# A hybrid decoder block on one core: Silu as one instruction, eight row buffers, and a rewritten passage between the projections and the up projections

## The chip, the core and the metric

The kernel runs on one core of a Trainium2 chip. A core has a matrix engine (PE, with PEld for its weight loads), a vector engine (DVE), a scalar engine that evaluates functions (ACT), GpSimd (POOL), and a sync engine (SP) that here only issues transfers. ACT issues transfers too: a transfer that stands in ACT's instruction list takes its turn there, and what stands behind it waits. Each engine works through its own list in order; semaphores join the lists. The metric is the device time of one execution in microseconds (us), as the median of several runs.

## What is computed

One layer over 16 meta tokens and 1024 real ones, D_MODEL 1024, everything float32:

```python
h = rmsnorm(concat([meta, x]), norm_g)
u_pool, z_pool, q, k, v, z_attn, f_logit, g_pool, g_attn = split(h @ w_in)
y_pool = causal_multiscale_pool(u_pool, pool_w, pool_scale) * silu(z_pool)
y_attn = forgetting_attention(q, k, v, log_sigmoid(f_logit + b)) * silu(z_attn)
merged = sigmoid(g_pool) * (y_pool @ w_up_pool) + sigmoid(g_attn) * (y_attn @ w_up_attn)
out = rmsnorm(x + merged @ w_out, final_norm_g)[meta rows dropped]
```

The pooling mixer takes, for each of four groups of 128 channels, a trailing mean over 2, 4, 8 or 16 positions minus the token itself, and then a 128x128 map. The attention has 8 heads of 64 channels; its softmax is divided by its row sums at the end.

## The kernel before

Matrix work is done on float32 split into a high and a low part, so each product takes three matmuls (`g_mm3`): high by high, high by low, low by high. A "raw" column block (`f_raw`, L281) is one of 24 blocks of 128 projected channels (four for each of `za` and `zp`, eight for each of `gp` and `ga`): 48 matmuls in two halves of 24, and each half is evicted from PSUM by an ACT copy into a staging tile `st` (L288) and stored to DRAM by SP (L289). Their PSUM tiles come from a pool of three, `pj`, so a half can begin only when the half three before it has been evicted. `f_u` stores the pooling input in the same way.

Attention fills the first two thirds of the time, with projections woven in as filler. Twenty raw blocks fit in there. The last four (`ga4` to `ga7`, the list `left`) run behind it and are PE's only work while the other engines prepare what the up projections need. This passage, L686 to L805, is where the change lies. In it:

- `reload` (L695) brings a stored row of z back from DRAM on ACT's queue, into a buffer of the tag "b", of which there are five.
- `silu_of` (L700) is a reload, a Sigmoid on ACT (L703) and a product on POOL (L704).
- `pool_pre` (L743) loads `u` on SP (L745), forms the window sums on DVE (L753, one to four adds) and the difference (L759), and splits it into `plh` (ACT, L762) and `pll` (DVE, L763). `pool_mm` (L715) runs 6 matmuls, then a DVE product with the gated z (L721), an ACT copy `yh` (L722) and a POOL difference `yl` (L723).
- The row sums are loaded, inverted (L728) and stored to DRAM as `recs`. `attn_out` (L731) loads the attention output `y` and two broadcast rows of reciprocals `rc` (L733, L737, both on ACT's queue), multiplies on DVE (L738), and gates on POOL (L740). L803 (ACT) and L804 (DVE) split the gated rows into `yah` and `yal`.
- `up(j, a)` (L820) loads and splits a weight block into `whu` (ACT, L826) and `wlu` (DVE, L827), reloads and squashes the gate, and runs 24 matmuls; `a` is 0 for the pooling branch, 1 for attention. The order is up(0,0), then up(j+1,0) and up(j,1) in turn.

PE's order is the order of the code. On the other engines a scheduler places the instructions by what they depend on; `after(ins, prev)` (L103) adds a dependence that only orders two instructions. In the kernel before, every Sigmoid is held behind the last Exp, so that ACT changes its function table once.

Of the kernel before, what the change touches and what calls it, by code (L numbers as in the profile page):

```python
# [8 lines left out]
F32 = mybir.dt.float32  # L9
# [5 lines left out]
D = 1024  # L15
# [39 lines left out]
def tile_hybrid_block(ctx, tc, x, meta, norm_g, w_in, b_forget, pool_w, pool_scale,  # L55
# [223 lines left out]
    spill = {}  # L279

    def f_raw(key, col):  # L281
        w = w_chunk(col)
        dt = dr.tile([128, SEQ], F32, name=f"sp_{key[0]}{key[1]}")
        spill[key] = dt
        for c0, c1 in HALVES:
            ps = yield from g_proj(w, NM + c0, NM + c1)
            st = stg.tile([128, 512], F32, name="st")
            nc.scalar.activation(st, ps, AF.Copy)  # L288
            nc.sync.dma_start(dt[:, c0:c1], st)  # L289
# [194 lines left out]
    pw = sm.tile([128, 4, 128], F32, name="pw", bufs=1)  # L484
# [197 lines left out]
    last_exp, last_dve = exps[-1], dves[-1]  # L682
# [6 lines left out]
    def after_exp(ins):  # L689
        after(ins, last_exp)  # L690

    def btile(name, dt=F32, tag="b"):
        return bp.tile([128, SEQ], dt, name=name, tag=tag, bufs=8 if tag == "y" else 5)
# [6 lines left out]
    def silu_of(key):  # L700
        z = reload(key)
        sg_ = btile("sg")
        after_exp(nc.scalar.activation(sg_, z, AF.Sigmoid))  # L703
        nc.gpsimd.tensor_tensor(z, z, sg_, op=ALU.mult)  # L704
        return z
# [9 lines left out]
    def pool_mm(zp, g, plh, pll):  # L715
        yh = btile("yh", F32R, "y")
        yl = btile("yl", F32R, "y")
        for c0, c1 in HALVES:
            ps = bank()
            run(g_mm3(ps, [(pwh[:, g], pwl[:, g], plh[:, c0:c1], pll[:, c0:c1])]))  # L720
            nc.vector.scalar_tensor_tensor(zp[:, c0:c1], ps, psc[:, g:g + 1], zp[:, c0:c1], op0=ALU.mult, op1=ALU.mult)  # L721
            nc.scalar.activation(yh[:, c0:c1], zp[:, c0:c1], AF.Copy)  # L722
            nc.gpsimd.tensor_tensor(yl[:, c0:c1], zp[:, c0:c1], r32(yh[:, c0:c1]), op=ALU.subtract)  # L723
        ypl[g] = (yh, yl)

    lall = sm.tile([128, 64], F32, name="lall", bufs=1)
    nc.sync.dma_start(lall, sums.rearrange("h (a b) -> (h a) b", b=64))
    nc.vector.reciprocal(lall, lall)  # L728
    nc.sync.dma_start(recs.rearrange("h (a b) -> (h a) b", b=64), lall)

    def attn_out(p):  # L731
        y = gp.tile([128, SEQ], F32, name="y", tag="g")
        nc.scalar.dma_start(y, spill["y", p])  # L733
        rc = btile("rc")
        for e in range(2):
            h = 2 * p + e
            nc.scalar.dma_start(rc[rows(e)[0]], recs[h:h + 1, :].to_broadcast([64, SEQ]))  # L737
        nc.vector.tensor_tensor(y, y, rc, op=ALU.mult)  # L738
        zs = silu_of(("za", p))
        nc.gpsimd.tensor_tensor(y, y, zs, op=ALU.mult)  # L740
        Y[p] = y

    def pool_pre(g):  # L743
# [16 lines left out]
        plh = gp.tile([128, SEQ], F32R, name="plh", tag="g")  # L760
        pll = gp.tile([128, SEQ], F32R, name="pll", tag="g")
        nc.scalar.activation(plh, u[:, NM:], AF.Copy)  # L762
        nc.vector.tensor_tensor(pll, u[:, NM:], r32(plh), op=ALU.subtract)  # L763
        return g, plh, pll

    made = [pool_pre(3), pool_pre(2)]
# [6 lines left out]
    def pooled():  # L773
        g, plh, pll = made.pop(0)
        pool_mm(zps.pop(0), g, plh, pll)

    zps = [silu_of(("zp", 3))]
    run(left[0])
    made.append(pool_pre(1))
    zps.append(silu_of(("zp", 2)))  # L780
    run(left[1])
    pooled()
    attn_out(0)
    made.append(pool_pre(0))
    zps.append(silu_of(("zp", 1)))
    run(left[2])
    pooled()
    attn_out(1)
    zps.append(silu_of(("zp", 0)))
    half_raw(left[3])  # L790
    pooled()
    pooled()
    run(left[3])
    attn_out(2)
    attn_out(3)
    HX.close()
    hq = ctx.enter_context(tc.tile_pool(name="hq", bufs=16, side="right", reuse_waits="tile"))

    ya = []
    for k in range(4):  # L800
        yh = hq.tile([128, SEQ], F32R, name="yah", tag="h")
        yl = hq.tile([128, SEQ], F32R, name="yal", tag="h")
        nc.scalar.activation(yh, Y[k], AF.Copy)  # L803
        nc.vector.tensor_tensor(yl, Y[k], r32(yh), op=ALU.subtract)  # L804
        ya.append((yh, yl))  # L805

    wo = {}

    def wo_chunk(k):
        raw = wp.tile([128, D], F32, name="rawo", tag="raw")  # L810
        nc.sync.dma_start(raw, wout[:, k, :])
        hi = hq.tile([128, D], F32R, name="woh", tag="h")
        lo = hq.tile([128, D], F32R, name="wol", tag="h")
        nc.scalar.activation(hi, raw, AF.Copy)
        nc.vector.tensor_tensor(lo, raw, r32(hi), op=ALU.subtract)
        wo[k] = (hi, lo)

    mg, gt = [], {}

    def up(j, a):  # L820
        y = (ypl, ya)[a]
# [7 lines left out]
        after_exp(nc.scalar.activation(sg_, sg_, AF.Sigmoid))  # L829
# [16 lines left out]
    up(0, 0)  # L846
    for j in range(8):
        if j < 7:
            up(j + 1, 0)
        up(j, 1)  # L850
# [77 lines left out]
```

## Time and profile before

| | |
|---|---|
| median of 3 runs | 799.39 us (798.90 to 800.28) |
| the profiled execution | 798.15 us, its span 796.40 us |
| PE busy | 765.2 us, 96% |
| DVE, ACT, POOL busy | 477.1, 394.7, 303.4 us |
| mean granted PE clock | 0.984 |

By stage (busy us in each stretch of the span):

| us from the start | PE | DVE | ACT | POOL | PE clock |
|---|---|---|---|---|---|
| 0 to 25, norm and first projections | 17.80 | 14.51 | 14.53 | 14.91 | 0.86 |
| 25 to 530, attention with filler | 502.60 | 329.43 | 286.01 | 194.23 | 1.00 |
| 530 to 571, first half of the passage | 41.00 | 27.68 | 13.95 | 16.71 | 1.00 |
| 571 to 612, second half of the passage | 25.64 | 23.65 | 18.06 | 37.70 | 0.87 |
| 612 to 701, up projections | 89.00 | 48.64 | 39.94 | 20.99 | 0.98 |
| 701 to 797, output projection | 89.13 | 33.21 | 22.21 | 18.82 | 0.97 |

How to read such rows: a timeline row gives the start, the duration, the engine, the line, the operation, output and input by the program's names, how many instructions the row joins, and in square brackets how long the engine had been idle before it and what ended that. A group row gives the least, the median and the greatest duration in nanoseconds. A PE row's end is modelled and laps over the next row's start, so distances are best taken from start to start. Rows with ACTq or SPq are the issuing of transfers, not their moving. The profiled execution is 1.75 us longer than its span, and 1.24 us shorter than the median.

### The profile page before, as it was taken

What the parts mean: (1) busy time and instruction counts of PE and PEld (TensorE: products, weight loads), DVE (VectorE), ACT (ScalarE), POOL (GpSimd) and SP (SyncE); (2) the same over time, 40 slices, a digit from 0 to 9 for tenths busy, and PEclk for the clock granted to TensorE, in tenths of its full rate; (3) what the DMA queues carried; (4) which work ended last, traced back from release to release, by engine and by line L of the source; (5) the groups of instructions that cost most, each with busy time, mean ns of one, the idle gap of its engine ahead of it and who ended that gap; (6) DMA issues with size and microseconds to landing.
All of it is one profiled execution on the core that took longest, in us unless ns stands there. A gap on an engine that the chain in (4) does not pass through costs nothing.

```text
span 796.4 us, 10658 instructions
## 1 busy us (share of the span) xinstructions
PE 765.2 (96%) x3893; PEld 653.1 (82%) x3893; DVE 477.1 (60%) x759; ACT 394.7 (50%) x755; POOL 303.4 (38%) x244
## 2 busy tenths in 40 slices
PE   6999999999999999999999999999695999999996
PEld 5897999988889888898888888888573888888885
DVE  4843566558568676586586675687637555434232
ACT  6652456457557564584475455643345445232121
POOL 5511225326316334253163172445588122222111
PEclk9999999999999999999999999999998999999998
DMA  9301122311321312313213223235474654533331
GB/s 298 90 5 51 28 90 71 94 53 47 92 68 27 86 47 68 86 34 85 86 43 99 74 67 87 73 113 188 165 257 135 198 181 162 185 106 106 106 107 53
DMA packets 74068, 79.86 MB, mean 100 GB/s; under 512 B 5504, under 2 KB 56704, under 8 KB 74016
## 3 DMA queue, kind: packets, MB, share of 16 engines
q1 hardware_dynamic: 68048, 59.79, 24.6%
q10 hardware_dynamic: 5968, 19.40, 7.7%
q8 instruction: 30, 0.49, 0.3%
q14 instruction: 22, 0.18, 0.1%
HBM read 58.10 MB, written 21.07 MB: 99 GB/s over the span
## 4 chain that ended last, share of the span: by engine, by line
PE 86%; DMA 5%; DVE 3%; issue 2%; POOL 2%; ACT 1%; SPq 0%; ACTq 0%; POOLq 0%; DVEq 0%
PE pj L140 61%; PE pj L862 11%; PE po L596 5%; PE ps L531 2%; PE ps L530 2%; DMA rl<-sp_za 2%; DVE s L753 1%; PE pj L446 1%; DMA u<-sp_u 1%; PE pt L551 1%; PE pt L559 1%; DMA gb<-in_norm_g_dram 1%; DMA y<-sp_y 1%; POOL rl L704 1%; POOL yl L723 1%
## 5 line engine op out<-in xcount | busy, mean ns | idle before, releaser
L140 PE MATMUL pj<-hh,whi 128*128 128x512 f32 (+4 forms) x768 | 183.0, 365 | 8.5 <-ACT st L288 6.0
L140 PE MATMUL pj<-hh,wlo 128*128 128x512 f32 (+4 forms) x768 | 180.1, 361 | 0.0
L140 PE MATMUL pj<-hl,whi 128*128 128x512 f32 (+4 forms) x768 | 179.7, 361 | 0.0
L129 POOL TENSOR_TENSOR wlo<-raw,whi 128x1024 fp32r<-128x1024 f32 x37 | 91.2, 2465 | 231.5 <-ACT whi L128 92.3
L140 PEld LDWEIGHTS pj<-hh,whi 128*128 128x128 f32 x768 | 132.3, 191 | 26.8 <-ACT st L288 6.5
L140 PEld LDWEIGHTS pj<-hl,whi 128*128 128x128 f32 x768 | 132.6, 190 | 17.9
L140 PEld LDWEIGHTS pj<-hh,wlo 128*128 128x128 f32 x768 | 131.9, 189 | 16.8
L580 DVE TENSOR_TENSOR pl<-S,ph 128x512 fp32r<-128x512 f32 (+4 forms) x112 | 93.8, 850 | 16.2 <-ACT ph L579 15.2
L588 POOL TENSOR_TENSOR acc<-acc,S 128x272 f32<-128x272 f32 (+4 forms) x80 | 77.1, 964 | 13.7 <-ACT S L576 8.3
L539 ACT ACTIVATE S<-ps,negc 128x400 f32<-128x400 f32 (+2 forms) x96 | 49.4, 515 | 55.3 <-DVE S L537 48.3
L575 DVE TENSOR_TENSOR S<-S,pt 128x512 f32<-128x512 f32 (+4 forms) x112 | 49.9, 498 | 21.4 <-PE pt L559 21.3
L576 ACT ACTIVATE S<-S 128x512 f32<-128x512 f32 (+4 forms) x112 | 48.5, 476 | 25.8 <-DVE S L575 25.7
L579 ACT ACTIVATE ph<-S 128x512 fp32r<-128x512 f32 (+4 forms) x112 | 52.8, 479 | 13.8 <-PE po L596 13.1
L546 DVE TENSOR_TENSOR m<-m,S 128x272 f32<-128x272 f32 (+4 forms) x80 | 40.6, 508 | 19.9 <-ACT S L539 18.2
L862 PE MATMUL pj<-wol,gh 128*128 128x512 f32 (+1 forms) x136 | 51.8, 381 | 0.0
L862 PE MATMUL pj<-woh,gh 128*128 128x512 f32 (+1 forms) x136 | 51.8, 381 | 0.0
L862 PE MATMUL pj<-woh,gl 128*128 128x512 f32 (+1 forms) x136 | 51.7, 380 | 0.0
L842 POOL TENSOR_TENSOR gl<-rl,gh 128x512 fp32r<-128x512 f32 x16 | 22.6, 1413 | 72.7 <-ACT gh L841 72.6
L128 ACT ACTIVATE whi<-raw 128x1024 fp32r<-128x1024 f32 x37 | 39.0, 1055 | 17.4 <-PE pj L140 16.1
L838 DVE TENSOR_TENSOR rl<-pj,rl 128x512 f32<-128x512 f32 x32 | 21.9, 688 | 35.1 <-PE pj L140 31.6
L288 ACT ACTIVATE st<-pj 128x512 f32<-128x512 f32 x48 | 28.4, 591 | 24.3 <-PE pj L140 23.8
L596 PE MATMUL po<-pl,V 128*128 128x512 f32 (+4 forms) x112 | 37.5, 335 | 0.0
(166 smaller groups left out, 1174.1 us busy)
## 6 DMA issues: line engine op xcount, KB each, us to landing
raw<-in_w_in_dram SPq DMA_DIRECT2D x40, 512.0 KB, 4.1
sp_gp<-st SPq DMA_DIRECT2D x16, 256.0 KB, 2.1
sp_ga<-st SPq DMA_DIRECT2D x16, 256.0 KB, 2.0
rl<-sp_gp ACTq DMA_DIRECT2D x8, 512.0 KB, 3.5
rl<-sp_ga ACTq DMA_DIRECT2D x8, 512.0 KB, 4.9
rawo<-in_w_out_dram SPq DMA_DIRECT2D x8, 512.0 KB, 4.8
xr<-in_x_dram SPq DMA_DIRECT2D x8, 512.0 KB, 4.3
xt<-in_x_dram SPq DMA_DIRECT2D x7, 512.0 KB
```

The lines of the kernel that those rows point to most:

```text
L128: nc.scalar.activation(hi, raw, AF.Copy)
L129: (eng or nc.gpsimd).tensor_tensor(lo, raw, r32(hi), op=ALU.subtract)
L140: nc.tensor.matmul(ps, a, b, start=(i == 0), stop=(i == len(seq) - 1))
L539: nc.scalar.activation(s[:kb, f0:], ps[:kb, f0:], AF.Identity, bias=nb_)
L546: nc.vector.tensor_tensor(m[:kb, c0:], m[:kb, c0:], s[:kb, c0:], op=ALU.max)
L575: nc.vector.tensor_tensor(s[:kb, c0:], s[:kb, c0:], self.pm[:kb, c0:], op=ALU.subtract)
L576: exps.append(nc.scalar.activation(s[:kb, c0:], s[:kb, c0:], AF.Exp))
L579: nc.scalar.activation(ph[:kb, c0:], s[:kb, c0:], AF.Copy)
L580: dves.append(nc.vector.tensor_tensor(pl[:kb, c0:], s[:kb, c0:], r32(ph[:kb, c0:]), op=ALU.subtract))
L588: nc.gpsimd.tensor_tensor(acc[:kb, c0:], acc[:kb, c0:], s[:kb, c0:], op=ALU.add)
L596: nc.tensor.matmul(self.po[:, c0:], v, r[:kb, c0:], start=(b == 0 and i == 0), stop=(b == self.nb - 1 and i == 1))
L862: nc.tensor.matmul(ps[:, :c1 - c0], mg[k][a][:, r], wo[k][b][:, c0:c1], start=(k == 0 and n == 0), stop=(k == KO - 1 and n == 2))
```

## The change

- **Silu.** `silu` is one ACT instruction in place. The Sigmoid on ACT with a POOL product, and the tile between them, are gone: eight products fewer on POOL. Silu and Sigmoid are not in one function table, so the built program has one more table load on ACT.
- **Buffers.** The tag "b" has eight buffers. All eight z rows (`zp`, `za`) are loaded ahead of the raw blocks, on ACT's queue. `pw`, a staging tile of the pooling map, now shares the attention tile `t`'s buffer.
- **Order of evictions.** Every Silu, gate Sigmoid and `plh` copy is held behind the latest eviction that was emitted before it (`evacs[-1]`) instead of behind the last Exp. `pool_pre` is cut into `pool_chain` and `pool_split`, placed between halves of raw blocks.
- **Attention rows.** `y` is loaded on SP early (`attn_in`) and gated on POOL first (`attn_gate`). The products with the reciprocals and the splits (`attn_out`) come behind up(0,0), and the eight `rc` loads go to SP, held behind the last store of the raw blocks.
- **Up projections.** Weights are loaded in a call of their own (`up_weights`), for the first two ahead of time, and the order is up(0,0), up(1,0), then up(j+2,0) and up(j,1) in turn: one more pooling block ahead of the first attention block.

```diff
 def f_raw(key, col):
-            nc.scalar.activation(st, ps, AF.Copy)
-            nc.sync.dma_start(dt[:, c0:c1], st)
+            evacs.append(nc.scalar.activation(st, ps, AF.Copy))
+            stores.append(nc.sync.dma_start(dt[:, c0:c1], st))
...
-    pw = sm.tile([128, 4, 128], F32, name="pw", bufs=1)
+    pw = ap_.tile([128, 4, 128], F32, name="pw", tag="t")
...
-        return bp.tile([128, SEQ], dt, name=name, tag=tag, bufs=8 if tag == "y" else 5)
+        return bp.tile([128, SEQ], dt, name=name, tag=tag, bufs=8)
...
-    def silu_of(key):
-        z = reload(key)
-        sg_ = btile("sg")
-        after_exp(nc.scalar.activation(sg_, z, AF.Sigmoid))
-        nc.gpsimd.tensor_tensor(z, z, sg_, op=ALU.mult)
-        return z
+    def silu(z):
+        after(nc.scalar.activation(z, z, AF.Silu), evacs[-1])
...
+    def attn_in(p):
+        y = gp.tile([128, SEQ], F32, name="y", tag="g")
+        nc.sync.dma_start(y, spill["y", p])
+        Y[p] = y
+
+    def attn_gate(p, zs):
+        ins = nc.gpsimd.tensor_tensor(Y[p], Y[p], zs, op=ALU.mult)
+        if p > 1:
+            after(ins, yls[-1])
+
     def attn_out(p):
-        y = gp.tile([128, SEQ], F32, name="y", tag="g")
-        nc.scalar.dma_start(y, spill["y", p])
         rc = btile("rc")
         for e in range(2):
             h = 2 * p + e
-            nc.scalar.dma_start(rc[rows(e)[0]], recs[h:h + 1, :].to_broadcast([64, SEQ]))
-        nc.vector.tensor_tensor(y, y, rc, op=ALU.mult)
-        zs = silu_of(("za", p))
-        nc.gpsimd.tensor_tensor(y, y, zs, op=ALU.mult)
-        Y[p] = y
+            after(nc.sync.dma_start(rc[rows(e)[0]], recs[h:h + 1, :].to_broadcast([64, SEQ])), stores[-1])
+        nc.vector.tensor_tensor(Y[p], Y[p], rc, op=ALU.mult)
+        yh = hq.tile([128, SEQ], F32R, name="yah", tag="h")
+        yl = hq.tile([128, SEQ], F32R, name="yal", tag="h")
+        nc.scalar.activation(yh, Y[p], AF.Copy)
+        nc.vector.tensor_tensor(yl, Y[p], r32(yh), op=ALU.subtract)
+        ya.append((yh, yl))
...
+    def pool_split(g):
+        u, plh, pll = chains[g]
+        after(nc.scalar.activation(plh, u[:, NM:], AF.Copy), evacs[-1])
+        return nc.vector.tensor_tensor(pll, u[:, NM:], r32(plh), op=ALU.subtract)
...
+    for p in range(3):
+        attn_in(p)
+    half_raw(left[0])
+    pool_split(3)
+    run(left[0])
+    split2 = pool_split(2)
+    silu(zp[3])
+    silu(zp[2])
+    lall = sm.tile([128, 64], F32, name="lall", bufs=1)
...
+    pool_chain(1)
+    half_raw(left[1])
+    silu(zp[1])
+    silu(zp[0])
+    run(left[1])
+    pooled(3)
+    silu(za[0])
+    silu(za[1])
+    attn_gate(0, za[0])
+    pool_split(1)
+    pool_chain(0)
+    attn_in(3)
+    half_raw(left[2])
+    silu(za[2])
+    silu(za[3])
+    attn_gate(1, za[1])
+    run(left[2])
+    pooled(2)
+    pool_split(0)
+    half_raw(left[3])
+    first_up = up_weights(0, 0)
+    pooled(1)
+    pooled(0)
+    run(left[3])
+    attn_gate(2, za[2])
...
+    attn_gate(3, za[3])
+    second_up = up_weights(1, 0)
...
-    up(0, 0)
+    up(0, 0, first_up)
+    for p in range(4):
+        attn_out(p)
+    up(1, 0, second_up)
     for j in range(8):
-        if j < 7:
-            up(j + 1, 0)
-        up(j, 1)
+        if j < 6:
+            up(j + 2, 0, up_weights(j + 2, 0))
+        up(j, 1, up_weights(j, 1))
```

The scheduler decides what this makes of the lists. Two places show it.

ACT's list in the last raw blocks, before. The three `st` rows are the evictions of `ga4`'s second half and of `ga5`'s two halves:

```order
L288 ACTIVATE st<-pj 128x512
L762 ACTIVATE plh<-u 128x1024
L697 DMA rl<-sp_zp_3066 128x1024
L733 DMA y<-sp_y_755 128x1024
L288 ACTIVATE st<-pj 128x512
L703 ACTIVATE sg<-rl 128x1024
L737 DMA rc<-recs 64x1024
L762 ACTIVATE plh<-u 128x1024
L288 ACTIVATE st<-pj 128x512
```

Between the last two of them stand a Sigmoid, a transfer of reciprocals and the split of a window sum.

The same place of ACT's list in the change; the three `st` are the two halves of `ga5` and the first of `ga6`:

```order
L288 ACTIVATE st<-pj 128x512
L698 ACTIVATE rl<-rl 128x1024 x2
L128 ACTIVATE whi<-raw 128x1024
L288 ACTIVATE st<-pj 128x512
L698 ACTIVATE rl<-rl 128x1024 x2
L715 ACTIVATE yh<-rl 128x512 x2
L762 ACTIVATE plh<-u 128x1024
L694 DMA rl<-sp_gp_3785 128x1024
L694 DMA rl<-sp_gp_3914 128x1024
L288 ACTIVATE st<-pj 128x512
```

`ga5`'s second eviction now has two Silu and a weight split ahead of it; the `plh` split and the wait that it brings stand behind it, ahead of `ga6`'s first eviction.

DVE's list around the first up projection, before: the products with the reciprocals (`y<-y,rc`) and a split of the attention rows stand ahead of up(0,0)'s `wlu`:

```order
L738 TENSOR_TENSOR y<-y,rc 128x1024
L721 SCALAR_TENSOR_TENSOR rl<-pj,psc,rl 128x512 x6
L738 TENSOR_TENSOR y<-y,rc 128x1024 x2
L804 TENSOR_TENSOR yal<-y,yah 128x1024
L827 TENSOR_TENSOR wlu<-rawu,whu 128x512
L804 TENSOR_TENSOR yal<-y,yah 128x1024 x3
L827 TENSOR_TENSOR wlu<-rawu,whu 128x512
```

And in the change, from the first product with a reciprocal on; the `wlu` of up(0,0), up(1,0) and up(2,0) all stand ahead of it, and one `rl<-pj,rl` and then the `wlu` of up(0,1) follow the last row:

```order
L734 TENSOR_TENSOR y<-y,rc 128x1024
L806 TENSOR_TENSOR rl<-pj,rl 128x512
L738 TENSOR_TENSOR yal<-y,yah 128x1024
L734 TENSOR_TENSOR y<-y,rc 128x1024
L806 TENSOR_TENSOR rl<-pj,rl 128x512
L734 TENSOR_TENSOR y<-y,rc 128x1024
L738 TENSOR_TENSOR yal<-y,yah 128x1024
L734 TENSOR_TENSOR y<-y,rc 128x1024
L738 TENSOR_TENSOR yal<-y,yah 128x1024
L806 TENSOR_TENSOR rl<-pj,rl 128x512
L738 TENSOR_TENSOR yal<-y,yah 128x1024
```

Four products with reciprocals, four splits and four products out of PSUM (`rl<-pj,rl`, counting the one that follows) moved behind three blocks of pooling work on PE.

96 lines of the change are left out of this document (36 added, 60 removed).

## The prediction

> **What bounds the kernel now.** I read the busy shares first, then the chain that ended last, then what PE waited for, and then the stage in which it waited.
>
> ```profile
> PE 765.2 (96%) x3893; PEld 653.1 (82%) x3893; DVE 477.1 (60%) x759; ACT 394.7 (50%) x755; POOL 303.4 (38%) x244
> ...
> PE 86%; DMA 5%; DVE 3%; issue 2%; POOL 2%; ACT 1%; SPq 0%; ACTq 0%; POOLq 0%; DVEq 0%
> ```
>
> PE carries the kernel. The change takes no matmul away, so all that it can win is time in which PE stands still. PE's waits show where:
>
> ```profile
> PE pj L140 <- DVE wlu L827: 7.1, 1, 7.1
> PE pj L140 <- ACT st L288: 6.0, 1, 6.0
> ...
> PE pj L140 <- ACT whu L826: 2.2, 1, 2.2
> ```
>
> Three single waits, 15.3 us, all in one stage, and there another engine is the busy one (the columns are PE, PEld, DVE, ACT, POOL, then granted clock, DMA share, GB/s):
>
> ```profile
> 571.00:612.00 41.00, 25.64 (x101) 19.64 (x100) 23.65 (x18) 18.06 (x24) 37.70 (x18) 0.87 0.57 179
> ```
>
> POOL works 37.70 of 41 us. PE's timeline around the three waits:
>
> ```profile
> 569.24 2.02 PE L140 MATMUL pj<-hh,wlo 128*128 128x512 f32 x8
> 577.29 3.60 PE L140 MATMUL pj<-hh,whi 128*128 128x512 f32 x8 [6.03 <-ACT st L288]
> 580.73 2.02 PE L140 MATMUL pj<-hl,whi 128*128 128x512 f32 x8
> ...
> 598.18 2.02 PE L140 MATMUL pj<-hh,wlo 128*128 128x512 f32 x8
> 602.37 1.20 PE L140 MATMUL pj<-yh,whu 128*128 128x512 f32 x4 [2.18 <-ACT whu L826]
> 603.41 1.10 PE L140 MATMUL pj<-yl,whu 128*128 128x512 f32 x4
> 611.65 2.07 PE L140 MATMUL pj<-yh,wlu 128*128 128x512 f32 x4 [7.14 <-DVE wlu L827]
> ...
> 614.99 1.10 PE L140 MATMUL pj<-yl,whu 128*128 128x512 f32 x4
> ...
> 622.45 1.10 PE L140 MATMUL pj<-yah,whu 128*128 128x512 f32 x4
> ...
> 628.05 1.10 PE L140 MATMUL pj<-yh,whu 128*128 128x512 f32 x4
> ```
>
> From 622.45 to 628.05 lie the 24 matmuls of one up projection: 5.60 us, 0.233 each, so 8 take 1.87 and 4 take 0.93. From start to start the first wait then costs 577.29 - (569.24 + 1.87) = 6.18, the second 602.37 - (598.18 + 1.87) = 2.32, the third 611.65 - (603.41 + 0.93) = 7.31. PE also runs slow behind them: 8 matmuls take 3.44 instead of 1.87 from 577.29 on, 8 take 3.34 from 611.65 on, and 4 take 1.04 instead of 0.93 behind the second wait: 1.57 + 1.47 + 0.11. Together **19.0 us**. The granted clock (third number from the end) shows the slow running as such:
>
> ```profile
> 577.20:580.80 3.60, 3.51 (x9) 2.80 (x10) 1.76 (x1) 2.62 (x5) 3.60 (x3) 0.53 0.85 244
> ...
> 602.30:603.40 1.10, 1.03 (x4) 0.86 (x5) 0.00 (x0) 0.97 (x2) 1.10 (x1) 1.00 0.70 160
> 611.60:615.00 3.40, 3.35 (x9) 2.68 (x10) 3.40 (x2) 1.14 (x2) 2.23 (x1) 0.55 0.36 89
> ```
>
> Behind 6.03 and 7.14 us of idling PE has half its clock for some 3.5 us, behind 2.18 us it keeps it; where between them the limit lies, no row shows. [...]
>
> **The first wait** (6.18 + 1.57). ACT's, DVE's and the chain's rows that lead to it:
>
> ```profile
> 563.77 6.21 DMA y<-sp_y
> 570.00 1.23 DVE L738 TENSOR_TENSOR y<-y,rc 128x1024 f32<-128x1024 f32 x1 [5.54 <-DMA y<-sp_y]
> 572.41 3.25 DVE L759 SCALAR_TENSOR_TENSOR u<-s,u 128x1024 f32<-128x1024 f32 x1
> 575.69 1.06 ACT L762 ACTIVATE plh<-u 128x1024 fp32r<-128x1024 f32 x1 [3.37 <-DVE u L759]
> 576.66 0.58 ACT L288 ACTIVATE st<-pj 128x512 f32<-128x512 f32 x1
> ```
>
> The load of an attention row holds DVE; behind it in DVE's list stands the last window sum, in ACT's list that sum's split, and behind the split the eviction that PE needs. The change loads `y` on SP ahead of the last raw blocks and puts the product with `rc` behind up(0,0), so that link is gone. In ACT's new list `ga5`'s second eviction has only four Silu and a weight split ahead of it. What is late next is `ga6`'s first eviction, behind pool group 3's `yh` and the window sum of `u1`. Its deadline: PE's `ga6` first half ends at 571.1; the second half (24 matmuls) and a pool product (6) bring it to 571.1 + 5.6 + 1.4 = 578.1, where `ga7` takes that PSUM buffer. Its earliest: going back by 5.6 and 1.4 from 571.1, `ga4`'s last half ends at 552.9; eviction and issues, 1.5 us; the load of `u1`; three DVE steps; two products out of PSUM, a `yh`, a split, two issues, the eviction, some 5 us.
>
> ```profile
> 534.61 6.99 DMA u<-sp_u
> ...
> L753 DVE TENSOR_TENSOR s<-u x4: 1233/1234/3355, 524.4 to 571.1; 128x1039 f32<-128x1039 f32 x4
> ```
>
> With 4 to 7.0 us for the load and 1.23 to 3.36 for each DVE step this gives 567 to 576.5, so 1.6 to 11 us in hand. I take this wait as gone.
>
> **The second and third wait** (2.32 + 0.11, and 7.31 + 1.47). What stood ahead of up(0,0)'s weights:
>
> ```profile
> 600.23 0.60 ACT L288 ACTIVATE st<-pj 128x512 f32<-128x512 f32 x1 [0.54 <-PE pj L140]
> 601.71 0.61 ACT L826 ACTIVATE whu<-rawu 128x512 fp32r<-128x512 f32 x1
> ...
> 603.98 1.58 DVE L738 TENSOR_TENSOR y<-y,rc 128x1024 f32<-128x1024 f32 x1 [4.22 <-issue]
> 605.48 3.37 DVE L804 TENSOR_TENSOR yal<-y,yah 128x1024 fp32r<-128x1024 f32 x1
> 608.77 2.82 DVE L827 TENSOR_TENSOR wlu<-rawu,whu 128x512 fp32r<-128x512 f32 x1
> ...
> 604.56 3.21 POOL L740 TENSOR_TENSOR y<-y,rl 128x1024 f32<-128x1024 f32 x1
> ```
>
> In the change `whu` and `wlu` of up(0,0) and up(1,0) are made during the raw blocks, ahead of every `rc`. Both waits go. But the attention rows must still be ready for up(0,1), which now comes after three pooling blocks, 3 x 5.60 = 16.8 us after the raw blocks end (call that T; 600.05 - 6.18 - 1.57 = 592.3), and its `wlu` is read 8 matmuls later, at T + 18.7. The rows:
>
> ```profile
> 598.71 1.10 ACTq L737 DMA_DIRECT2D rc<-recs x2
> ...
> L738 DVE TENSOR_TENSOR y<-y,rc x4: 1226/1470/2233, 570.0 to 604.0; 128x1024 f32<-128x1024 f32 x4
> L804 DVE TENSOR_TENSOR yal<-y,yah x4: 1210/2288/3391, 605.5 to 616.0; 128x1024 fp32r<-128x1024 f32 x4
> ...
> L838 DVE TENSOR_TENSOR rl<-pj,rl x32: 672/690/692, 617.7 to 703.4; 128x512 f32<-128x512 f32 x32
> ```
>
> The last eviction ends 0.78 after the raw blocks (600.23 + 0.60 - 600.05). Then SP issues the store (some 0.4) and the eight `rc` loads that are held behind it, at 0.55 each. In the rows before, a pair issued at 598.71 let DVE start at 603.98, 5.27 us. So DVE starts at T + 6.4. Its list has four products (1.23), four splits (1.21), four products out of PSUM (0.69), a wait for the first `yah` (0.4) and the `wlu` (0.68): 13.6 us, ready at T + 20.0. PE wants it at T + 18.7: **1.3 us** of new waiting. ACT has room: `yah` three is done near T + 14, the `whu` near T + 16. The unknown is how fast eight `rc` loads go together, and whether DVE meets POOL. Below, nothing is late; above, the first pair comes one more landing (4 us, the difference of 5.27 and an issue) later, which makes 5.3, and a slow restart of 1.5 with it. I take 2.5, near the rows' 1.3, for the loads share their way with seven others. [...]
>
> The two gates (2.4 to 3.2 each on POOL) must be over by T + 6.4. Pool group 0's matmuls end 23 matmuls before T, at T - 5.4; a product (1.4), a `yh` (0.6) and two to four POOL differences (1.3 each, half of a full row's 2.4) follow, and the gates end at T + 4 to T + 8.5. The rows show what a meeting costs: the split beside POOL's 3.21 took 3.37 instead of 1.21. [...]
>
> **What else moves.** Eight Sigmoid become eight Silu on ACT. No row shows a Silu; its nearest is the Sigmoid.
>
> ```profile
> L703 ACT ACTIVATE sg<-rl x8: 1057/1062/1064, 540.3 to 606.0; 128x1024 f32<-128x1024 f32 x8
> L703 ACT ACT_TABLE_LOAD  x1: 1283/1283/1283, 537.2 to 537.2; - x1
> L704 POOL TENSOR_TENSOR rl<-rl,sg x8: 2400/2596/3392, 541.5 to 607.7; 128x1024 f32<-128x1024 f32 x8
> ...
> rl<-sp_za ACTq DMA_DIRECT2D x4, 512.0 KB, 7.3
> ```
>
> I take 1.06 each, nothing new; at twice that ACT has 8.5 us more in a passage where it is idle 23 of 41 us, which hides it. The second table load, 1.28 us, comes behind the last eviction and ends with two gate Sigmoid at T + 4.2, while ACT then waits until T + 7.6 for the first attention row; without that cover it costs 1.28. POOL loses 8 x 2.60 = 20.8 us of products in the passage that it filled, which is the reason why I expect DVE's short durations. Eight z loads on ACT's list cost eight issues and may hold evictions (a rival, below). `pw` shares a buffer that is first written at the end of the first attention unit, long after its split. The new order of up blocks has as many matmuls.
>
> **The sum.** 796.40 - 19.0 + 2.5 = 779.9 of span; the profiled execution is 1.75 above its span (798.15), so 781.7, and the median of the runs shown is 1.24 above that one (799.39): **782.9 us**.
>
> **The rivals.**
> - *The first wait returns one half later* (15%). ACT stands at `yh` behind DVE's `u1` chain while `ga6`'s first eviction stands behind it. For it: the same pattern as before, and the late end of the margin is 1.6 us. Against: POOL has left DVE's way, and `u1` is loaded far from the end. At the size of the wait before, cut by the time in hand, 4 us plus the restart of 1.57: 788.5.
> [...]
> - *Slower* (3%): the z loads stand in ACT's list ahead of evictions, and the last two Silu ahead of `ga6`'s second one, due at 578.1 + 5.6 = 583.7. They start near 532. Should the eight come one by one, X apart, that eviction is done at 532 + 8X + 2.3, and PE loses 8X - 49.4. Above X = 8.8 this eats the 19.0 and 1.6 more; at 9.5 it gives 799.4 - 19.0 + 26.6 = 807. Against it: one load lands in 7.3 us with others under way, and 179 GB/s move 512 KB in 2.9.
> - *The gain does not come* (3%): Silu's and the early loads' order leaves another engine's wait of the same size in the stage, 799.
>
> **How the numbers follow.** Forecast 72%: 779.5 (no new wait, and a median as near its profile as this one's) to 786.5 (the upper bound of the new wait). Taking in the two rivals of 788.5 and 789.2, the range is 779.5 to 790, which leaves out 6%; were it to end at 786.5 it would leave out over a quarter. A measurement of this kernel tells about 0.2% (1.6 us) from no change. Faster: 72 + 15 + 7 = 94%; the same 3%; slower 3%.
>
> **What would show it.** Right: PE's waits on `st` and up(0,0)'s `whu` and `wlu` gone, POOL well under 30 us busy in that stage, the clock 1.00 through it, one wait of 1 to 4 us on `wlu` or `yal` at the first attention block. Wrong: a wait on `st` or `pll` of several us near the pool products, a granted clock near 0.5 anywhere after 530, DVE splits of 3 us beside a POOL gate behind the raw blocks, or ACT idle on a z load while an eviction stands behind it.

## The result, and the profile after

The changed kernel takes 780.40 us (median of 4 runs, 780.07 to 780.79), the kernel before on the same chip 799.84 us (798.90 to 800.83): a ratio of 0.9757, 95% interval 0.974 to 0.9774. The forecast was 782.9 within 779.5 to 790.0. The profiled execution took 780.58 us with a span of 778.9; forecast for the span were 779.9.

Busy times and PE's waits of the changed kernel:

```profile
PE 760.6 (98%) x3893; PEld 650.9 (84%) x3893; DVE 460.2 (59%) x759; ACT 394.7 (51%) x756; POOL 282.3 (36%) x236
...
PE pj L140 <- ACT whu L789: 0.9, 1, 0.9
PE pj L140 <- DVE wlu L790: 0.7, 1, 0.7
```

PE does the same work in a span 17.5 us shorter. POOL lost 21.1 us, nearly all of it the eight products (8 x 2.60 = 20.8). The three waits on `st`, `whu` and `wlu` of 15.3 us are gone, and two small ones are left. The stage in which they lay, in the columns of before (PE, PEld, DVE, ACT, POOL, then granted clock):

```profile
571.00:612.00 41.00, 39.96 (x170) 31.34 (x168) 26.03 (x27) 21.35 (x27) 18.48 (x11) 1.00 0.57 166
```

PE was busy for 25.64 of these 41 us and is now for 39.96, at a clock of 1.00 instead of 0.87. POOL went from 37.70 to 18.48. The rows that matter in this stage, in order of time:

```profile
557.89 2.01 ACT L698 ACTIVATE rl<-rl 128x1024 f32<-128x1024 f32 x2
...
566.53 5.75 POOL L725 TENSOR_TENSOR y<-y,rl 128x1024 f32<-128x1024 f32 x2
...
568.97 3.67 ACTq L694 DMA_DIRECT2D rl<-sp_gp  x2
572.74 0.60 ACT L288 ACTIVATE st<-pj 128x512 f32<-128x512 f32 x1 [4.33 <-POOL y L725]
...
592.72 4.95 SPq L733 DMA_DIRECT2D rc<-recs  x8
...
598.41 1.22 DVE L734 TENSOR_TENSOR y<-y,rc 128x1024 f32<-128x1024 f32 x1
...
607.23 1.10 PE L140 MATMUL pj<-yh,wlu 128*128 128x512 f32 x4
...
607.62 1.06 ACT L797 ACTIVATE rl<-rl 128x1024 f32<-128x1024 f32 x1 [1.66 <-DMA rl<-sp_gp]
608.58 0.61 ACT L789 ACTIVATE whu<-rawu 128x512 fp32r<-128x512 f32 x1
609.10 1.04 ACT L737 ACTIVATE yah<-y 128x1024 fp32r<-128x1024 f32 x1
...
609.25 1.45 PE L140 MATMUL pj<-yah,whu 128*128 128x512 f32 x4 [0.92 <-ACT whu L789]
610.53 1.42 PE L140 MATMUL pj<-yal,whu 128*128 128x512 f32 x4
612.65 1.20 PE L140 MATMUL pj<-yah,wlu 128*128 128x512 f32 x4 [0.71 <-DVE wlu L790]
```

Two Silu take 2.01 us together, as two Sigmoid do where they are kept (2.01 in the run with all but Silu). At the first attention block PE starts 609.25 - (607.23 + 0.93) = 1.09 late, the first four matmuls take 0.35 too long (they read the fourth row's split, which ends at 610.14), the next four 1.19 and the four on `wlu` 0.11: 2.74 us, where 2.5 was forecast. Three things stand in ACT's list there: it waits 1.66 us for the load of up(2,0)'s gate, and behind that gate stand the weights of up(0,1) and the fourth row's split. And at 572.74 there is a near miss: ACT stood 4.33 us at the issue of two gate loads, whose buffers come free when POOL has gated the attention rows, with `ga6`'s first eviction behind them. PE wanted that buffer at 577.5, 4.2 us after the eviction ended at 573.3.

### The profile page after: what moved, and what is told of

It is laid out like the page before. It is cut to its first block, busy times and chain, and to the rows that moved or that the text cites. A ratio compares the mean times of both kernels' runs of the same rounds, so it can differ in the third digit from the quotient of the medians.

```text
span 778.9 us, 10637 instructions
## 1 busy us (share of the span) xinstructions
PE 760.6 (98%) x3893; PEld 650.9 (84%) x3893; DVE 460.2 (59%) x759; ACT 394.7 (51%) x756; POOL 282.3 (36%) x236
## 4 chain that ended last, share of the span: by engine, by line
PE 92%; DMA 2%; POOL 2%; DVE 1%; ACT 1%; issue 1%; SPq 0%; POOLq 0%; DVEq 0%
PE pj L140 66%; PE pj L886 11%; PE po L596 5%; PE ps L531 3%; PE ps L530 2%; DMA rl<-sp_gp 1%; PE pj L446 1%; PE pt L551 1%; PE pt L559 1%; DMA gb<-in_norm_g_dram 1%; POOL yl L716 1%; DMA rc<-recs 1%; DVE xt L175 1%; PE pt L616 0%; PE pj L250 0%
## 5 line engine op out<-in xcount | busy, mean ns | idle before, releaser
L901 ACT ACTIVATE sq<-xr 128x512 f32<-128x512 f32 (+1 forms) x17 | 10.3, 608 | 53.9 <-DVE xr L900 53.9
```

## The experiments

Two theories. The **order theory** is the prediction's: PE waited because an eviction and two weight splits stood behind attention-row work in the lists of ACT and DVE, and the new order takes them out; POOL's relief only makes DVE's steps short. The **POOL theory**: the stage was POOL's (37.70 of 41 us). Its eight products of 2.60 held buffers, loads and DVE steps, and what won the time is that they are gone. The kernel before took 798.73 to 799.46 us (medians) on the chips of these runs; each time has the ratio to it.

**Silu alone**, on the kernel before:

```diff
-        sg_ = btile("sg")
-        after_exp(nc.scalar.activation(sg_, z, AF.Sigmoid))
-        nc.gpsimd.tensor_tensor(z, z, sg_, op=ALU.mult)
+        after_exp(nc.scalar.activation(z, z, AF.Silu))
```

> The kernel before with Silu as one instruction and nothing else changed. Order theory (PE waited because an eviction and a weight split stood behind attention-row work in ACT's and DVE's lists): the lists stay, so two waits stay in smaller form; DVE's steps beside POOL fall from 3.25 to 1.22 (first wait, 2.0 less) and from 3.37 and 2.82 to 1.21 and 0.68 (third wait, 4.3 less, and its slow restart of 1.47 with it): 799.8 - 7.8 = 792, 788 to 796. POOL theory (the stage was POOL's, 37.70 of 41 us, and the 20.8 us of products taken off it are the gain): 784 or less, no wait over 2 us left.

784.71 us, ratio 0.9831 (0.9811 to 0.9852): 14 us from three lines. The order theory missed by 7. The POOL theory missed by 0.7, and one wait of 2.76 us is left where it had none over 2. First the kernel before at the first wait, then this one, with two rows of its third wait at the end:

```profile
560.60 2.78 POOL L704 TENSOR_TENSOR rl<-rl,sg 128x1024 f32<-128x1024 f32 x1 [1.85 <-ACT sg L703]
...
563.41 0.32 ACTq L697 DMA_DIRECT2D rl<-sp_zp  x1
563.77 0.44 ACTq L733 DMA_DIRECT2D y<-sp_y  x1
```

```profile
558.93 0.33 ACTq L731 DMA_DIRECT2D y<-sp_y  x1
...
562.39 1.22 DVE L736 TENSOR_TENSOR y<-y,rc 128x1024 f32<-128x1024 f32 x1
...
569.25 1.23 DVE L757 SCALAR_TENSOR_TENSOR u<-s,u 128x1024 f32<-128x1024 f32 x1
...
571.47 0.58 ACT L288 ACTIVATE st<-pj 128x512 f32<-128x512 f32 x1
...
573.66 2.71 PE L140 MATMUL pj<-hh,whi 128*128 128x512 f32 x8 [2.76 <-DVE rl L719]
...
597.65 1.78 DVE L825 TENSOR_TENSOR wlu<-rawu,whu 128x512 fp32r<-128x512 f32 x1
...
599.49 0.73 PE L140 MATMUL pj<-yh,wlu 128*128 128x512 f32 x2 [0.84 <-DVE wlu L825]
```

In the kernel before, the issue of the `zp` load begins right when POOL's product ends (563.38), and the load of `y` stands behind it. Without the product `y` is issued 4.8 us earlier, its product with `rc` runs at 562.39 instead of 570.00, the last window sum takes 1.23 instead of 3.25, and the eviction runs 5.2 us earlier. DVE's list has the same order here as before. ACT's has not: the scheduler has put the loads of `zp` (550.18) and `y` ahead of an eviction and a `plh` (559.69, 560.17) behind which they stood. In the kernel before, that `plh` starts at 561.14, so waiting for POOL's buffer explains at most 2.3 of the 4.8 us (563.41 - 561.14); how the rest divides between the new place in the list and the shorter steps of DVE, no run shows.

The third wait shrinks with its order almost kept: all four products with `rc` still stand ahead of up(0,0)'s `wlu` on DVE (the last at 595.82; one split that stood there too now comes behind it), and PE waits 0.84 us for `wlu` instead of 7.14, and 0.35 once more.

**All but Silu**: the changed kernel with Sigmoid and POOL's product again.

```diff
-        after(nc.scalar.activation(z, z, AF.Silu), evacs[-1])
+        sg_ = btile("sg", F32, "y")
+        after(nc.scalar.activation(sg_, z, AF.Sigmoid), evacs[-1])
+        nc.gpsimd.tensor_tensor(z, z, sg_, op=ALU.mult)
```

> The changed kernel with each Silu put back as a Sigmoid and a POOL product, everything else kept. Order theory: the wait on the eviction does not come back; POOL's list from 555 on has three weight splits (2.4), eight products (2.4), two gates, eight differences (1.3) and two gates, 46 us against some 37 until up(0,0), so its differences end about 4 us late at up(0,0) and its last gates meet two to four of DVE's splits at 2.4 each: 780.4 + 4 + 5, 786 to 793. POOL theory: all of the gain goes, 796 to 800.

789.39 us, ratio 0.9884 (0.9866 to 0.9902). The number lies where the order theory had it, and the POOL theory, by which all of the gain goes, is off by 6.6. The first wait is back, though its old link is gone; the second and third are not:

```profile
577.73 1.26 POOL L718 TENSOR_TENSOR yl<-rl,yh 128x512 fp32r<-128x512 f32 x1
578.95 2.34 POOL L727 TENSOR_TENSOR y<-y,rl 128x1024 f32<-128x1024 f32 x1
...
579.02 2.62 ACTq L694 DMA_DIRECT2D rl<-sp_gp  x2
581.75 0.60 ACT L288 ACTIVATE st<-pj 128x512 f32<-128x512 f32 x1 [9.17 <-POOL y L727]
...
582.40 3.78 PE L140 MATMUL pj<-hh,whi 128*128 128x512 f32 x8 [4.63 <-ACT st L288]
...
600.44 1.19 PE L140 MATMUL pj<-yl,whu 128*128 128x512 f32 x4 [0.37 <-POOL yl L718]
```

It is the near miss of the changed kernel, 9 us later: the two gate loads can be issued when POOL's steps end, at 578.99 and 581.29, and the eviction stands behind them. At up(0,0) PE waits 0.37 us for POOL's `yl` and not at all for `whu` or `wlu`: for the second and third wait the new order is enough, without Silu.

**The same, with those two loads taken out of ACT's list**, to see whether the place in the list or POOL is the bound:

```diff
-        sg_ = reload((("gp", "ga")[a], j))
+        sg_ = reload((("gp", "ga")[a], j), nc.gpsimd if (j, a) in ((0, 0), (1, 0)) else nc.scalar)
```

> The changed kernel with Sigmoid and POOL's product again (789.39 us), and the loads of the first two gates issued from POOL's list instead of ACT's. In 789.39 ACT stood 9.17 us ahead of ga6's first eviction, at the issue of those two loads, whose buffers POOL's steps free; PE lost 4.81 us there and 2.65 at a reduced clock. The eviction could run at 572.6 instead of 581.75. Order theory (an eviction stood behind a held instruction in ACT's list, POOL itself has room): the wait on the eviction goes and 5 to 7.5 us with it: 782 to 784.5 us. POOL theory (POOL has no idle time between 558 and 607 there, and its products stand ahead of the yl that up(0,0) reads): PE only arrives earlier at up(0,0) and waits there for yl, 5 to 7 us where it was 0.37: 788 to 791 us, the wait moved and nothing won.

790.72 us, ratio 0.9901 (0.9884 to 0.9917). The eviction now runs at 572.40 and nothing is won:

```profile
570.70 3.39 POOL L129 TENSOR_TENSOR wlo<-raw,whi 128x1024 fp32r<-128x1024 f32 x1
...
574.12 0.38 SPq L788 DMA_DIRECT2D rawu<-in_w_up_pool_dram  x1
574.55 0.50 SPq L745 DMA_DIRECT2D u<-sp_u  x1
...
578.96 3.46 DVE L753 TENSOR_TENSOR s<-u 128x1039 f32<-128x1039 f32 x1 [7.15 <-DMA u<-sp_u]
...
589.20 0.79 PE L140 MATMUL pj<-plh,pwh 128*128 128x512 f32 x1 [5.52 <-DVE rl L716]
```

PE waits 5.52 us one stop further on, as the POOL theory had it in time, though not at `yl`: a weight load on SP waits for the buffer that POOL's `wlo` split empties (it ends at 574.09, behind four products), the last `u` stands behind that load, and the DVE steps of its sum take 3.46 and 3.28 us, where they took 2.24 and 2.21 in the changed kernel. Moving these two loads changed where PE waits, not how long. The new wait again stands behind a place in a list, SP's; what taking that load out of the way too would win, no run shows.

**The kernel before with its products on DVE**:

```diff
-        nc.gpsimd.tensor_tensor(z, z, sg_, op=ALU.mult)
+        nc.vector.tensor_tensor(z, z, sg_, op=ALU.mult)
```

> The kernel before (798.7 us) with its eight z products on DVE instead of POOL, Sigmoid and all loads as they were. POOL theory (what Silu alone won, 14 us, is POOL's 20.8 us of products and the buffers, loads and DVE instructions that stood behind them; DVE has 17 of 41 us free and needs 1.23 each, 9.8 in all): most of Silu's gain comes without Silu, 785 to 790 us. Order theory (Silu won because ACT and the buffers have one step fewer; DVE's list, in which the eviction's link stands, only gets longer): 797 to 803 us, the wait on ga6's first eviction still 4 us or more.

787.81 us, ratio 0.9859 (0.9832 to 0.9887), in the POOL theory's range: 11 to 12 of Silu's 14 us come without Silu, with more work on DVE and the same transfers on the same engines. The tile between Sigmoid and product is still there, so the buffer that Silu frees can account for no more than the rest. POOL is busy for 24.30 of the 41 us instead of 37.70. Here too the scheduler changed ACT's list a little: the load of `y` (557.84) now stands ahead of that of `zp` (558.96).

**Moving only the first link** of the kernel before: the first product with `rc` and its loads behind the last window sum, POOL's products kept.

```diff
-        nc.vector.tensor_tensor(y, y, rc, op=ALU.mult)
+        after(nc.vector.tensor_tensor(y, y, rc, op=ALU.mult), plls[-1])
...
-    attn_out(0)
+    plls = []
...
+    attn_out(0)
```

> The kernel before with the first product with the reciprocals, and its row's load, put behind the last window sum. Order theory: the wait of 6.18 on the eviction and its restart of 1.57 go, the third wait stays or grows by up to 3: 799.8 - 7.7 to - 4.7, 792 to 796. POOL theory: POOL's work is as before, 799.8 within 1.6.

796.51 us, ratio 0.9971 (0.996 to 0.9982), between the ranges of the two theories: 2 of the 7.75 us that the prediction put down to this link. Three waits on `st` are left, up to 2.1 us, the attention rows come later (5.2 on `yah`), and 2.5 on `yh` is new.

**The changed kernel without the order of evictions**: Silu and gate Sigmoid behind the last Exp, `plh` free.

```diff
-        after(nc.scalar.activation(z, z, AF.Silu), evacs[-1])
+        after(nc.scalar.activation(z, z, AF.Silu), last_exp)
...
-        after(nc.scalar.activation(plh, u[:, NM:], AF.Copy), evacs[-1])
+        nc.scalar.activation(plh, u[:, NM:], AF.Copy)
...
-        after(nc.scalar.activation(sg_, sg_, AF.Sigmoid), evacs[-1])
+        after(nc.scalar.activation(sg_, sg_, AF.Sigmoid), last_exp)
```

> The changed kernel with Silu and gate Sigmoid held behind the last Exp only, and the plh copies not held, instead of behind the latest eviction. Order theory: ga5's weight split comes behind a Silu and ga4's last eviction, some 3 us of waiting on it, and a gate Sigmoid that waits for its load comes ahead of ga5's second eviction, 4 to 6 us with a slow restart of 1.6: 785 to 793. POOL theory: POOL's work is the same, so 780.4 within 1.5.

787.67 us, ratio 0.9861 (0.9845 to 0.9876): here the order theory is right, and this edit carries 7.3 us, more than Silu alone leaves to win (784.71 to 780.40).

```profile
549.01 1.28 ACT L698 ACT_TABLE_LOAD   x1
550.30 1.06 ACT L698 ACTIVATE rl<-rl 128x1024 f32<-128x1024 f32 x1
551.27 1.04 ACT L762 ACTIVATE plh<-u 128x1024 fp32r<-128x1024 f32 x1
554.12 0.60 ACT L288 ACTIVATE st<-pj 128x512 f32<-128x512 f32 x1 [1.81 <-DMA sp_ga<-st]
...
555.56 1.05 ACT L128 ACTIVATE whi<-raw 128x1024 fp32r<-128x1024 f32 x1
...
556.65 2.50 PE L140 MATMUL pj<-hh,whi 128*128 128x512 f32 x8 [3.75 <-ACT whi L128]
```

With eight z rows loaded early, all Silu are ready early. Unheld, the table load and two Silu, a `plh` and an eviction that waits for an earlier store stand ahead of the weight split that PE wants, which ran at 548.70 in the changed kernel and runs at 555.56 here. PE waits once more at 578.18, 1.67 us for a product out of PSUM. In this kernel the hold keeps the early Silu out of the way.

**The attention rows and the up weights back in the program's order of before**, on the changed kernel:

```diff
-            after(nc.sync.dma_start(rc[rows(e)[0]], recs[h:h + 1, :].to_broadcast([64, SEQ])), stores[-1])
+            nc.sync.dma_start(rc[rows(e)[0]], recs[h:h + 1, :].to_broadcast([64, SEQ]))
...
-    first_up = up_weights(0, 0)
...
-    second_up = up_weights(1, 0)
...
-    up(0, 0, first_up)
     for p in range(4):
         attn_out(p)
-    up(1, 0, second_up)
+    up(0, 0, up_weights(0, 0))
+    up(1, 0, up_weights(1, 0))
```

> The changed kernel (780.4 us) with the attention rows and the up weights back in the order of before: rc loads not held behind the last store, the rows emitted ahead of the first up block, its weights not made ahead. Order theory: wlu of up(0,0) stands behind the four products with rc on DVE again, so PE waits there; in the kernel before that cost 11.2 us with its slow restart, and with POOL relieved each product, split and landing is shorter by up to half: 784 to 790 us, the wait named for wlu or whu at the first up block. POOL theory (those steps were long only beside POOL's products; without them the rows and weights are there in time in either order): 780.4 within 1.5.

781.45 us, ratio 0.9774 (0.9746 to 0.9801), the POOL theory's number. PE waits neither for `whu` nor for `wlu` at the first up block; one wait of 2.33 on `st` at 587.41 stands in place of the 2.74 at the first attention block, with a slow restart (clock 0.53 from 589.80 to 592.00). This edit is worth about 1 us at most, not 11.2. But it does not bring back the list of before: the scheduler places up(0,0)'s `wlu` (579.32) behind one product with `rc` only, and the other three at 582.37 and from 595.36 on. So the order theory's condition was not met here. What decides is Silu alone, where all four products stand ahead of that `wlu` and PE waits 0.84 us for it.

**The z rows loaded pair by pair** ahead of their Silu:

```diff
-    for z, key in ((zp, "zp"), (za, "za")):
-        for g in range(4):
-            z.append(reload((key, 3 - g if key == "zp" else g)))
-    zp.reverse()
+    zp, za = [None] * 4, [None] * 4
...
+    zp[3], zp[2] = reload(("zp", 3)), reload(("zp", 2))
...
+    zp[1], zp[0] = reload(("zp", 1)), reload(("zp", 0))
...
+    za[0], za[1] = reload(("za", 0)), reload(("za", 1))
...
+    za[2], za[3] = reload(("za", 2)), reload(("za", 3))
```

> The changed kernel (780.4 us) with each pair of z rows loaded just ahead of its Silu pair in the program's order, instead of all eight first; the lists of ACT and SP differ in a few places near the loads only. Both theories: the loads were hidden, 780.4 within 1. Should the early loads carry a part of the gain (buffers claimed early, DMA that is later free for y and u), 783 or more, with a wait on a Silu, an eviction or a product out of PSUM.

780.85 us, ratio 0.9765 (0.9735 to 0.9795): no difference, and the same two waits of 0.9 and 0.7. The scheduler moved the loads only a few places, so this is weak evidence on much later loads.

**Two pooling blocks ahead of the first attention block** instead of three:

```diff
-    up(1, 0, second_up)
     for j in range(8):
-        if j < 6:
-            up(j + 2, 0, up_weights(j + 2, 0))
+        if j < 7:
+            up(j + 1, 0, up_weights(j + 1, 0) if j else second_up)
```

> The changed kernel (780.4 us) with two pooling up blocks ahead of the first attention block instead of three. Order theory as in the prediction (the attention rows are ready near T + 19, whatever PE does): PE reaches the first attention block 5.6 us earlier, at 602.6 by the trace of the changed kernel, and the fourth row is there at about 608 without the gate of up(2,0) ahead of it; the wait grows from 2.7 us to about 6 with a slow restart of 1.5: 785 us (783 to 788), the wait named for ACT yah or DVE yal. Rival (the rows only follow PE, since their splits queue behind what PE's results release): 780.4 within 1.5.

787.34 us, ratio 0.9858 (0.9843 to 0.9873), 0.66 below the top of the order theory's range and 2.3 above its value.

```profile
607.25 1.06 ACT L797 ACTIVATE rl<-rl 128x1024 f32<-128x1024 f32 x1 [1.61 <-DMA rl<-sp_ga]
...
608.73 1.04 ACT L737 ACTIVATE yah<-y 128x1024 fp32r<-128x1024 f32 x1
...
609.82 0.80 PE L140 MATMUL pj<-yah,whu 128*128 128x512 f32 x1 [3.63 <-ACT yah L737]
```

The rows do not follow PE: PE is ready for them at 602.3 instead of 608.2, and the fourth row's split comes 0.4 earlier. It comes no earlier because another gate's load (`sp_ga`, up(0,1)'s own) took the place of the one the expectation left out.

**The gate of up(2,0) behind the fourth row's split**:

```diff
-        after(nc.scalar.activation(sg_, sg_, AF.Sigmoid), evacs[-1])
+        after(nc.scalar.activation(sg_, sg_, AF.Sigmoid), lastyah[0] if (j, a) == (2, 0) else evacs[-1])
```

> The changed kernel with the Sigmoid of up(2,0)'s gate held behind the fourth attention row's split on ACT. Order theory: in the changed kernel ACT stood 1.66 us at that gate's load, with the fourth row (ready at 607.12, split at 609.10) and the weights of up(0,1) behind it. Now the row is split at 607.1, the gate follows at 608.1, the weights at 609.1; PE starts the first attention block at 609.7 instead of 609.25, but yal and wlu are there when it wants them: 1.5 us lost instead of 2.74, so 779.2 us (778.3 to 780). Rival (the waits were the row's own, its reciprocals landing late): 780.4 within 0.6.

780.47 us, ratio 0.9771 (0.9756 to 0.9786): no gain in the time, where 779.2 was forecast. In the trace the wait did shrink:

```profile
527.23 0.23 PE L596 MATMUL po<-ph,V 128*128 128x144 f32 x1
...
608.07 1.10 PE L140 MATMUL pj<-yh,wlu 128*128 128x512 f32 x4
610.58 1.19 PE L140 MATMUL pj<-yah,whu 128*128 128x512 f32 x4 [1.41 <-ACT whu L789]
```

PE loses 610.58 - (608.07 + 0.93) = 1.58, and 0.10 in the four matmuls: 1.68 instead of 2.74, forecast 1.5. But the matmul quoted first, in code that the edit does not touch, came at 526.39 in the changed kernel and comes at 527.23 here: the kernel's start varies by as much as this edit wins, and four runs of each cannot show it in the median. From that matmul to the span's end it takes 778.7 - 527.23 = 251.47 us, against 778.9 - 526.39 = 252.51 in the changed kernel: 1.04 less, as the wait says.

**The same, with the `rc` loads held behind the last store but one**:

```diff
-            after(nc.sync.dma_start(rc[rows(e)[0]], recs[h:h + 1, :].to_broadcast([64, SEQ])), stores[-1])
+            after(nc.sync.dma_start(rc[rows(e)[0]], recs[h:h + 1, :].to_broadcast([64, SEQ])), stores[-2])
```

> As the run with the gate behind the rows, and the eight rc loads held behind the last half's store but one instead of the last, so some 2.8 us earlier (half of the 5.6 us between two evictions, since two stores leave per eviction of 128x1024). Order theory: the fourth row is split near 604.5 and the weights of up(0,1) near 606.5, ahead of 608.2 where PE wants them; both waits of 2.74 us go: 777.7 us (777.2 to 779). Against it DVE takes the first product with rc ahead of wlu for up(1,0): if the rc loads still land 8 us after their issue, that wlu comes late and PE waits at up(1,0) instead, 780 to 783. The theory that the attention rows' loads, not the gate, set the time puts all the gain of this pair here and none in the run with the gate alone.

779.95 us, ratio 0.9765 (0.975 to 0.9779), 0.95 above the order theory's range. The wait at the first attention block is gone and another has come:

```profile
593.21 3.43 DVE L734 TENSOR_TENSOR y<-y,rc 128x1024 f32<-128x1024 f32 x1
...
606.26 1.28 DVE L790 TENSOR_TENSOR wlu<-rawu,whu 128x512 fp32r<-128x512 f32 x2
...
606.99 1.20 PE L140 MATMUL pj<-yh,wlu 128*128 128x512 f32 x4 [1.47 <-DVE wlu L790]
```

Five of the eight loads went 7.4 us earlier (issued from 585.31 on) and not 2.8, since each half has one eviction and one store and the last store but one belongs to the half before. So DVE's second product came at 593.21, a time at which POOL's gates run in the changed kernel (590.73 to 595.95), and took 3.43 us instead of 1.22, and the weights of up(2,0) came behind the rows.

**And with those weights made ahead of the fourth row**:

```diff
-    for p in range(4):
+    for p in range(3):
         attn_out(p)
     up(1, 0, second_up)
+    third_up = up_weights(2, 0)
+    attn_out(3)
     for j in range(8):
         if j < 6:
-            up(j + 2, 0, up_weights(j + 2, 0))
+            up(j + 2, 0, up_weights(j + 2, 0) if j else third_up)
```

> The run with the rows two us earlier (779.95 us), and the weights of up(2,0) made ahead of the fourth attention row; there PE lost 1.74 us at wlu of up(2,0), which stood at 606.26 behind three products, three splits and four results on DVE, and nothing at the first attention block. Order theory: wlu of up(2,0) comes right behind the first split of a row, near 603.5, and PE does not wait for it; the fourth row's split ends near 610 to 611 and is wanted at 610: 778.2 us (777.7 to 779.4). If instead every engine's list is full and the steps only change places, 779.95 within 0.5.

778.32 us (777.99 to 778.36), ratio 0.9734 (0.9709 to 0.9759), 0.1 from the expected value, and the fastest kernel of the study. Its ratio overlaps that of the changed kernel; its four times do not (780.07 to 780.79 there). In this stage PE stands still no more:

```profile
571.00:612.00 41.00, 41.00 (x179) 33.27 (x178) 29.19 (x29) 22.13 (x28) 21.79 (x11) 1.00 0.66 196
...
526.85 0.23 PE L596 MATMUL po<-ph,V 128*128 128x144 f32 x1
```

From the matmul quoted there to the span's end it takes 776.6 - 526.85 = 249.75, 2.76 less than the 252.51 of the changed kernel, the whole wait of 2.74.

## Why the prediction was right, and where it was not

*The size of the gain* was right: 19.0 us of PE's time could be won, all of it went, and 2.74 came back for a forecast of 2.5. The span is 1.0 below the forecast (779.9); 0.46 of that lies ahead of the passage (the fixed matmul came at 526.85 before and at 526.39 after), where one profiled execution differs from the next by up to 1.2 us. The step from the profiled execution to the median failed: 1.24 us were added since the execution of before lay below its median by that, and this one lies 0.18 above its own. Both make up the 2.5 us by which 782.9 was too high. The ends of the range do not follow from the terms named for them: without a new wait the sum gives 780.4 (779.2 with a median at its profiled execution) and not 779.5, and with a new wait of 5.3 and its restart 787.2 and not 786.5.

*Which edit wins it* was wrong in part. The step that failed is the relief of POOL, taken only as a reason for short DVE steps and given no microsecond of its own. Silu alone wins 14.0 us, and all else alone 9.3; together they win 19.4, so the two overlap. The sum of the three waits came out right since, with everything done at once, it does not matter who is credited.

*The first wait* was put down to a product with `rc` ahead of the last window sum. That link was in the chain, but moving it alone wins 2.2 us, and taking it out of the way with POOL's products kept brings the wait back on another link (4.63 us). "What is late next" was looked for in the `u1` chain and given 1.6 to 11 us; that chain ended at 564.29, well in time. What was next are the gate loads in ACT's list, which the prediction counted as issues without asking which engine frees their buffers. POOL does. That the 4.2 us in hand lie between 1.6 and 11 is luck, since they come from another chain; with the products there are none.

*The second and third wait* were said to go because `whu` and `wlu` are made ahead of every `rc`. That was right, but not the only way: with POOL's products kept the new order takes both waits away (0.37 us on `yl` is left), and with Silu alone the old order leaves 0.84 and 0.35 of them. Either is enough, and so this part of the gain cannot be credited to one of them.

*The new wait* was right in size and half right in cause. DVE starts at T + 7.0 (598.41, T is 591.43) for T + 6.4, and the gates are over at T + 4.5, within T + 4 to T + 8.5, so they were out of the way when DVE started. The forecast's 789.2 stands for both gates meeting DVE and has 4.8 us more waiting than the 2.5, and no run shows the 4.8: what the traces show of one meeting is 2.16 us, for a split of 3.37 instead of 1.21 beside a gate of 3.21 in the kernel before. Nor does a run show that 2.5 us at a stretch cost no restart, as the forecast has it: in the changed kernel the waits came apart, 0.92 and 0.71 us at a clock of 1.00, and with Silu alone 2.76 us at a stretch cost 1.6 more. "`whu` near T + 16" was T + 17.2, behind the gate of up(2,0): its wait for a load was not in the working, and moving it takes 1.06 of the 2.74 away.

*What was costed at nothing* is so: Silu takes 1.0 each, the second table load is hidden (ACT loads a table for Silu at 556.60 and one for the gate Sigmoid at 592.29, 1.28 us each, and PE waits behind neither), and the z loads are, as far as a move of a few places shows (780.85). The order of evictions, given no term either, costs 7.3 us if it is left out; that it would be worth nothing without the early loads is argued from the trace, and no run of the changed kernel leaves out both.

## What to carry to other kernels

When one engine is busy nine tenths of a stage, as POOL was here (37.70 of 41 us), give its relief a term of its own: follow every list in which an instruction waits for a buffer that this engine frees, loads above all, since what stands behind it is named in the profile for another reason. Here moving POOL's work away won 14.0 us, and 11 to 12 even onto an engine that then has more to do; a new order around it won 9.3, and moving one or two instructions around it 2.2 us or nothing. Where several edits of one change each look sufficient, their gains need not add (here 14.0 and 9.3 alone, 19.4 together), so test each alone in both directions. And where a scheduler places the instructions, read the lists that it built before calling a run a test of their order: one edit that put the program's order back did not put the engine's order back.

## What the runs showed of the hardware

PE's clock fell behind shorter idling than the 6.03 and 7.14 us of the prediction's rows. With Silu alone PE idled 2.76 us (the granted clock is the third number from the end):

```profile
573.60:576.20 2.60, 2.54 (x9) 2.04 (x10) 0.67 (x2) 2.21 (x3) 1.85 (x2) 0.76 0.78 221
576.20:579.00 2.80, 2.80 (x9) 2.23 (x8) 0.68 (x1) 1.54 (x2) 0.67 (x1) 0.61 0.53 152
```

With the rows back in the program's order of before it idled 2.33:

```profile
587.40:589.80 2.40, 2.39 (x8) 1.93 (x9) 1.03 (x2) 1.59 (x3) 1.85 (x2) 0.72 0.94 336
589.80:592.00 2.20, 2.20 (x7) 1.74 (x6) 0.48 (x1) 0.67 (x2) 2.20 (x3) 0.53 0.64 203
```

And with the products kept and the gate loads off ACT's list, after 1.85:

```profile
618.80:620.50 1.70, 1.62 (x4) 1.29 (x5) 1.48 (x3) 1.70 (x3) 0.00 (x0) 0.58 0.43 125
```

With the first link moved, four matmuls took 1.88 us instead of 0.93 behind 2.52 us of idling (601.69 to 603.57), but the clock stayed at 1.00 behind 2.07; with the products on DVE four took 1.04 and the next four 0.94 behind 2.00. In the kernel before the clock stayed at 1.00 behind 2.18 us, and behind 1.41 in the run with the gate behind the rows. So between 1.85 and 2.18 us it went either way in these runs, and the slow stretch need not begin with the first matmul: in the second pair of rows the matmuls start 0.23 to 0.34 us apart up to 588.45, and only from there, 1.04 us behind the restart, 0.41. The prediction put no restart on a wait of 2.5; with Silu alone 2.76 us of waiting cost 1.6 more.

In the changed kernel the eight broadcast loads of `rc` were issued in a row, 0.5 to 0.7 us apart. The first two had landed when DVE began the product that reads them (598.41), so at most 5.7 and 5.2 us after their issue; the seventh, the only one whose landing the trace tells, took 8.1. In the kernel before the second of a pair took 4.0, and in the run with the rows earlier, where they were issued as five and three, one took 4.4.

And the first 526 us, which these edits do not touch, differ by up to 1.2 us from one profiled execution to the next (a fixed matmul at 526.09 with one up block less, at 527.30 with the rows earlier): a gain of 1 us is better read between two points of the trace than from medians of four.
